# RWKV triangles inverted from 16x16 substitution and 32x32 products, transposed by TensorE

## The chip, the core and the metric

The kernel runs on one core of one Trainium2 chip. TensorE multiplies matrices into PSUM, VectorE, ScalarE and GpSimd work elementwise, and SyncE issues the DMAs. The metric is the device time of one execution in microseconds. Shorter is better; the median of the runs is compared.

## The reference

The reference is one block of a hybrid model on 512 latent tokens and 256 context tokens of width 1024: a projection, three mixers (RWKV7 in both directions, a convolution, an mLSTM), a gated merge, and an MLP. The change concerns the RWKV mixer alone, which runs this recurrence for 8 heads of size 64, forward and backward, first over the context and then, from its state, over the latents:

```python
def step(S, inp):
    w_t, k_t, v_t, kk_t, a_t = inp[:5]
    S = (S * w_t[:, :, None, :]
         - jnp.einsum('bhvk,bhk->bhv', S, kk_t)[..., None] * (kk_t * a_t)[:, :, None, :]
         + v_t[..., None] * k_t[:, :, None, :])
    y = jnp.einsum('bhvk,bhk->bhv', S, inp[5]) if emit else None
    return S, y
```

## The kernel before

The recurrence is cut into 12 chunks of 64 tokens (8 latent, 4 context). Within a chunk the 64 updates are tied together by a 64x64 unit triangle of inner products, which the kernel inverts; a chunk's effect on the state is then a few matrix products. Two heads make a pair j (0 to 3); forward and backward direction lie in the lower and the upper 64 partitions of a tile.

For a pair, `ctx` and `lat` load the operands, `gram` forms the inner products and masks them, `transposed` turns the keys around, and `invert` inverts 48 triangles (2 directions, 2 heads, 12 chunks) at once. Each 64x64 triangle is handled as two diagonal blocks of 32x32 and one block off the diagonal. VectorE transposes the diagonal blocks so that the chunks lie along the free axis within each partition (L1012), solves them by 30 steps of substitution, two operations each (L1017, L1019), transposes what the off-diagonal products need (L1022, L1024), and transposes the result back (L1042); TensorE only forms the off-diagonal blocks (L1033, L1034, L1048, L1049), and ScalarE moves them out of PSUM.

`chain` walks the 12 chunks of a pair in 36 steps, three for each chunk: a product with the state (L1100), the product with the inverted triangle TT (L1106), and the product that makes the next state (L1115), with ScalarE copies between (L1104, L1109) and a sum on VectorE at the end (L1116). `output` forms the results (L1081, L1082).

`weave(j)` sets the order: at each step of `chain(j)` it asks for a number of pieces of the preparation of pair j + 1 (`lat`, with `gram` and `invert`, then `ctx` of pair j + 2; the table PACE says how many pieces, one piece ends at each `yield`), and for some three matmuls of the merge gates (`gates`, L512), 100 spread over the steps and 20 at the end. The chain has a raised priority, and the other pieces are tied behind the chain's last instruction. A scheduler then puts each engine's instructions into one order, which that engine follows. Three stages, j = 0, 1, 2, prepare the next pair; the fourth runs beside the conv branch's norm and the modulation weights. Pair 0 is prepared earlier, between the heads of the mLSTM (`front`, `back`, whose operations are at L262 and from L788 to L858).

The gate products need weights that are split in two: ScalarE rounds (L152) and GpSimd forms the difference (L153). GpSimd also scales the chain's state (L1113) and the keys (L995).

## Time and profile before

| | us |
|---|---|
| median of 3 runs | 1371.11 |
| lowest, highest | 1370.52, 1717.46 |
| profiled execution | 1377.12 |
| its span, first to last instruction | 1375.3 |
| busy in it: TensorE, VectorE, GpSimd, ScalarE | 1252.9, 849.2, 585.7, 511.8 |

The profile is one execution, some 6 us above the median. Busy time is the union of an engine's records; records of matmuls overlap, since the next one starts before the last one has left the array. A window's row gives the busy time of each engine in that stretch, the granted TensorE clock as a share of full speed, and the load of the DMA engines. The chain of waits is followed back from the last instruction, at each step to whatever released it.

### The profile page before, as it was taken

Reading aid. Unit: us, or ns where it says so; the run is one execution under the profiler, and the core shown is the slowest. Engines: PE = TensorE matmul, PEld = TensorE weight load, DVE = VectorE, ACT = ScalarE, POOL = GpSimd, SP = SyncE. Lnnn points to the kernel's source line nnn. Section 1 sums busy time; section 2 is a strip of 40 time slices with the busy share of each in tenths; the row PEclk is TensorE's granted clock in tenths of the full one; section 3 lists DMA queues with packets and bytes.
Section 4 is the critical chain, followed back from the end, with each engine's and each line's share of the span. In section 5 each row is a group of like instructions: output and inputs, shape, how many; then the busy total and the mean of one; then the engine's idle time right before and its main releaser. Section 6 shows DMA issues by size and latency. Waiting matters only on the chain.

```text
span 1375.3 us, 21700 instructions
## 1 busy us (share of the span) xinstructions
PE 1252.9 (91%) x8004; PEld 969.6 (71%) x8004; DVE 849.2 (62%) x1509; ACT 511.8 (37%) x1048; POOL 585.7 (43%) x547
## 2 busy tenths in 40 slices
PE   6999989786999886999899988889999999999997
PEld 1587877565888775667566665667888878888886
DVE  2599588889266993797977857678366534300202
ACT  4434556632222231243342444422354444322322
POOL 0443334426755441332433435533456544444442
PEclk9999999898999997999998998999999999999999
DMA  9221588732633314323431244787434433433422
GB/s 375 65 69 58 134 270 255 246 104 62 186 99 97 111 64 120 110 93 101 143 110 49 85 145 136 259 263 249 131 112 156 142 100 95 153 104 96 131 95 89
DMA packets 101457, 187.85 MB, mean 137 GB/s; under 512 B 10708, under 2 KB 29396, under 8 KB 100328
## 3 DMA queue, kind: packets, MB, share of 16 engines
q1 hardware_dynamic: 101352, 186.47, 42.9%
q8 instruction: 63, 1.03, 0.3%
q14 instruction: 42, 0.34, 0.1%
HBM read 148.64 MB, written 29.40 MB: 129 GB/s over the span
## 4 chain that ended last, share of the span: by engine, by line
PE 45%; DVE 14%; DMA 5%; issue 3%; ACT 1%; POOL 1%; SPq 0%; DVEq 0%; POOLq 0%; ACTq 0%
PE pt L1268 16%; PE pd L1337 13%; PE dg L512 5%; DMA wad<-wada 4%; DVE N L1019 3%; DVE tmp L1017 2%; PE pg L973 2%; PE ch L1100 1%; PE pd L682 1%; DVE N L1012 1%; PE ch L1106 1%; DVE accm L608 1%; PE dl L262 1%; PE pbk L998 1%; PE ch L1115 1%
## 5 line engine op out<-in xcount | busy, mean ns | idle before, releaser
L153 POOL TENSOR_TENSOR wlo<-raw,whi 128x512 fp32r<-128x512 f32 x296 | 435.5, 1477 | 555.5 <-ACT whi L152 488.9
L152 ACT CAST whi<-raw 128x512 fp32r<-128x512 f32 x296 | 182.0, 618 | 318.7 <-PE pt L1268 118.8
L262 PE MATMUL dl<-hh,wlo 128*128 128x512 f32 (+1 forms) x368 | 149.7, 407 | 10.8 <-POOL wlo L153 10.8
L262 PE MATMUL dl<-hh,whi 128*128 128x512 f32 (+1 forms) x368 | 151.4, 412 | 2.7 <-ACT kT L758 1.9
L262 PE MATMUL dl<-hl,whi 128*128 128x512 f32 (+1 forms) x368 | 148.5, 403 | 0.0
L1337 PE MATMUL pd<-h2l,whi 128*128 128x512 f32 (+1 forms) x272 | 103.3, 381 | 0.7 <-POOL h2l L1320 0.7
L1337 PE MATMUL pd<-h2h,wlo 128*128 128x512 f32 (+1 forms) x272 | 102.7, 379 | 0.0
L1337 PE MATMUL pd<-h2h,whi 128*128 128x512 f32 (+1 forms) x272 | 101.5, 380 | 0.2 <-ACT h2h L1317 0.2
L1363 DVE TENSOR_TENSOR x<-pt,modb 128x512 f32<-128x512 f32 x8 | 5.5, 690 | 154.7 <-PE pt L1268 154.7
L1268 PE MATMUL pt<-whi,h1h 128*128 128x512 f32 x256 | 99.6, 389 | 0.0
L1268 PE MATMUL pt<-whi,h1l 128*128 128x512 f32 x256 | 99.6, 389 | 0.0
L1268 PE MATMUL pt<-wlo,h1h 128*128 128x512 f32 x256 | 99.1, 389 | 0.0
L262 PEld LDWEIGHTS dl<-hh,wlo 128*128 128x128 f32 (+1 forms) x368 | 70.7, 192 | 26.0 <-POOL wlo L153 11.2
L262 PEld LDWEIGHTS dl<-hh,whi 128*128 128x128 f32 (+1 forms) x368 | 71.2, 193 | 18.6 <-ACT kT L758 2.1
L262 PEld LDWEIGHTS dl<-hl,whi 128*128 128x128 f32 (+1 forms) x368 | 70.8, 192 | 15.2 <-issue 1.5
L608 DVE SCALAR_TENSOR_TENSOR accm<-wad,sc,accm 128x512 f32<-128x512 f32 x56 | 59.1, 1056 | 35.2 <-DMA wad<-wada 34.6
L1113 POOL TENSOR_TENSOR sps<-SV,PL 64x128 f32<-64x128 f32 x88 | 40.0, 454 | 85.1 <-DVE SV L1116 81.9
L1341 DVE TENSOR_TENSOR relu<-relu 128x512 f32<-128x512 f32 x32 | 38.9, 1218 | 55.8 <-ACT relu L1340 55.7
L512 PE MATMUL dg<-hl,whi 128*128 128x512 f32 x144 | 66.5, 462 | 0.0
L512 PE MATMUL dg<-hh,whi 128*128 128x512 f32 x144 | 65.7, 456 | 0.0
L512 PE MATMUL dg<-hh,wlo 128*128 128x512 f32 x144 | 65.6, 456 | 0.0
L1019 DVE TENSOR_TENSOR N<-N,tmp 128x30 f32<-128x30 f32 (+14 forms) x120 | 58.1, 484 | 3.0
(389 smaller groups left out, 2792.3 us busy)
## 6 DMA issues: line engine op xcount, KB each, us to landing
raw<-wblk SPq DMA_DIRECT2D x296, 256.0 KB, 2.9
wad<-wada SPq DMA_DIRECT2D x64, 256.0 KB, 4.0
wada<-wada SPq DMA_DIRECT2D x8, 1024.0 KB, 13.4
BK<-kb SPq DMA_DIRECT2D x16, 384.0 KB, 5.2
sp_bk<-BK SPq DMA_DIRECT2D x8, 768.0 KB, 5.2
BK<-sp_bk SPq DMA_DIRECT2D x8, 768.0 KB, 4.1
sp_g<-gt SPq DMA_DIRECT2D x24, 256.0 KB, 2.0
sp_al<-al SPq DMA_DIRECT2D x8, 640.0 KB, 4.6
```

The costliest lines, as they stand in the source:

```text
L152: A.copy(hi[:, :], raw[:, :])
L153: G.tensor_tensor(lo[:, :], raw[:, :], hi[:, :], ALU.subtract)
L262: PE.matmul(ps_[0:M, :], lhsT=w[:, ko:ko + M], rhs=x[seg][:, k, :], start=(n == 0), stop=(n == 3 * KT - 1))
L512: yield lambda w=w, x=x, k=k, ko=ko, n=n: PE.matmul(ps[:, :], lhsT=w[:, ko:ko + P], rhs=x[:, k, :], start=(n == 0), stop=(n == 3 * KT - 1))
L608: V.scalar_tensor_tensor(o, t[:, :], sc[:, k, 0:1], o, ALU.mult, ALU.add)
L973: PE.matmul(ps[hf, i, :, :], lhsT=BK[dd, c, x, :], rhs=al[:, c] if lat else AL[d][dd, 8 + c:9 + c, :], start=True, stop=True)
L1017: V.tensor_tensor(tv, N[:, s + 1:32, s:s + 1].to_broadcast([P, n, s]), N[:, s:s + 1, 0:s].to_broadcast([P, n, s]), ALU.mult)
L1019: V.tensor_tensor(N[:, s + 1:32, 0:s], N[:, s + 1:32, 0:s], tv, ALU.add)
L1113: last["Pool"] = G.tensor_tensor(sps[hf], SV[d][hf, c, :, :], PL[hf, c, :].unsqueeze(2).to_broadcast([64, 2, CH]), ALU.mult)
L1268: PE.matmul(pss[i][:, :], lhsT=x[:, k, ts_], rhs=w[:, :], start=(k == 0 and n == 0), stop=(k == nk - 1 and n == 2))
L1337: PE.matmul(ps[:, ts_], lhsT=w[:, ko:ko + P], rhs=x[:, k, ts_], start=(k == 0 and n == 0), stop=(k == 7 and n == 2))
L1341: V.tensor_tensor(t[:, :], t[:, :], t[:, :], ALU.mult)
```

## The change

The substitution now runs on 16x16 blocks, in 14 steps of two operations, and on all of them at once. N gets its transposed form by TensorE: products of the masked Gram blocks with slices of the identity into PSUM, and two ScalarE copies into N. The inverted 16x16 diagonal blocks come back in the same way, once as D and once transposed as Dt. GpSimd multiplies LT by a mask that clears the 16x16 diagonal blocks. With L the rest of the 32x32 block, I + L D is formed in PSUM and multiplied by D, which gives the inverse of the 32x32 block; its transpose is formed by further products. The blocks off the 32x32 diagonal follow by the same two products as before. Copies from PSUM are shared between ScalarE and VectorE.

`gram` now collects in one PSUM bank the products of both directions that stay in their own half of the partitions (`own`), and in a second bank those that go to the other half (`oth`); the first are masked by one operation over 128 partitions, into LT, which holds the former LR as its second half. The masks change with it. The first pair now uses the bank "m" as the second bank, later pairs a bank of the chain's pool. The tables PACE, DENSE and EXTRA stay as they are, and `invert` and `gram` yield fewer pieces. LR, TN and most of tmp go, and the mLSTM's result yc takes a buffer of gbc in turn. The constants loaded at the start grow by 64 columns.

```diff
@@ -46,7 +46,7 @@
 NBLK = 148
-CONST_ORDER = [("ident", 128), ("bones", 128), ("gmf", 128), ("gmb", 128), ("nmf", 128), ("nmb", 128)]
+CONST_ORDER = [("ident", 128), ("bones", 128), ("gmo", 128), ("gmx", 128), ("dm", 64), ("nmf", 128), ("nmb", 128)]
@@ -88,15 +88,15 @@
     SY.dma_start(par[:, :], params)
-    cst = K.tile([P, 512], F32, name="cst")
-    SY.dma_start(cst[:, :], consts[:, 0:512])
+    cst = K.tile([P, CO["nmf"]], F32, name="cst")
+    SY.dma_start(cst[:, :], consts[:, 0:CO["nmf"]])
     def CN(name):
-        return cst[:, CO[name]:CO[name] + 128]
+        return cst[:, CO[name]:min(CO[name] + 128, CO["nmf"])]
@@ -854,7 +854,7 @@
             PE.transpose(pt[:, c * 128:(c + 1) * 128], ht[:, c, :], ident)
-        yc = S.tile([P, NT], F32, tag="yc", name="yc")
+        yc = S.tile([P, NT], F32, tag="gbc", name="yc", bufs=2)
@@ -878,16 +878,16 @@
             self.BK = [S.tile([P, NCH, 2, CH], F32, name=f"BK{h}") for h in range(2)]
-        self.LT.append(S.tile([P, 32, CH], F32, name=f"LT{i}"))
-        self.tc.nc.gpsimd.memset(self.LT[i][:, 24:32, :], 0.0)
+        self.LT.append(S.tile([P, 2, 24, CH], F32, name=f"LT{i}"))
                 self.AL[d].append(S.tile([P, 20, CH], F32, name=f"AL{d}{i}{h}"))
-            self.LR.append(S.tile([P, 8, CH], F32, name=f"LR{i}{h}"))
         if i == 0:
-            self.tmp = S.tile([P, 256], F32, name="tmp")
-            self.N = S.tile([P, 32, 32], F32, name="N")
-            self.TN = S.tile([P, 32, 32], F32, name="TN")
+            self.tmp = S.tile([P, 112], F32, name="tmp")
+            self.N = S.tile([P, 1056], F32, name="N")
+            self.tc.nc.gpsimd.memset(self.N[:, :], 0.0)
+            self.D, self.Dt = (S.tile([P, 24, 32], F32, name=x) for x in ("D", "Dt"))
@@ -895,15 +895,15 @@
         PS = self.ea.enter_context(tc.tile_pool(name="psa", bufs=1, space=PSUM, side="right", reuse_waits="tile"))
-        self.PS, self.PG = PS, [PS]
-        self.AL, self.LR, self.LT, self.BKt = [[], []], [], [], []
+        self.PS, self.PG = PS, (PS, "m")
+        self.AL, self.LT, self.BKt = [[], []], [], []
         self.PSC = self.es.enter_context(tc.tile_pool(name="psb", bufs=1, space=PSUM, reuse_waits="tile"))
-        self.PG.append(self.PSC)
+        self.PG = (self.PSC, "g")
@@ -954,41 +954,40 @@
     def gram(self, j, h, quarters):
         nc, HF = self.tc.nc, self.HF
         V, PE = nc.vector, nc.tensor
-        AL, LR, BKt, BK = self.head(j, h)
+        AL, BKt, BK = self.head(j, h)
         LT = self.LT[j % 2]
-        gm = [self.CN("gmf"), self.CN("gmb")]
         for c4 in quarters:
+            lat = c4 < 2
+            w = 2 if lat else 1
+            own, oth = (pool.tile([P, 4, w, CH], F32, tag=tag, name="pg") for pool, tag in ((self.PS, "g"), self.PG))
+            for i in range(4):
+                c = c4 * 4 + i
+                for x, ps in enumerate((own, oth)):
+                    for d in range(2):
+                        dd, hf = HF[d], HF[(d + x) % 2]
+                        al = AL[d][dd, 0:16, :].rearrange("p (x c) t -> p c x t", x=2)[:, c] if lat else AL[d][dd, 8 + c:9 + c, :]
+                        PE.matmul(ps[hf, i, :, :], lhsT=BK[dd, c, x, :], rhs=al, start=True, stop=True)
+            mo, mx = (self.CN(n)[:, (2 - w) * CH:2 * CH].rearrange("p (x t) -> p x t", t=CH).unsqueeze(1).to_broadcast([P, 4, w, CH])
+                      for n in ("gmo", "gmx"))
+            g = h * 12 + c4 * 4
+            dst = LT[:, ::-1, g:g + 4, :] if lat else LT[:, 0:1, g:g + 4, :]
+            V.tensor_tensor(dst.rearrange("p x c t -> p c x t"), own[:, :, :, :], mo, ALU.mult)
+            yield
             for d in range(2):
-                dd, od = HF[d], HF[1 - d]
...
-                yield
+                od = HF[1 - d]
                 if lat:
                     dst = AL[d][od, 0:16, :].rearrange("p (x c) t -> p c x t", x=2)[:, c4 * 4:c4 * 4 + 4]
                 else:
                     dst = AL[d][od, 16:20, :].unsqueeze(2)
-                V.tensor_tensor(dst, ps[od], m_[od], ALU.mult)
+                V.tensor_tensor(dst, oth[od], mx[od], ALU.mult)
                 yield
     def transposed(self, j, h, quarters):
         nc = self.tc.nc
         A, G, PE = nc.scalar, nc.gpsimd, nc.tensor
-        AL, LR, BKt, BK = self.head(j, h)
+        AL, BKt, BK = self.head(j, h)
         for c4 in quarters:
             cs = slice(c4 * 4, c4 * 4 + 4)
             pl = self.PL[:, j, cs, h:h + 1].unsqueeze(3).to_broadcast([P, 4, 2, CH])
@@ -1000,61 +999,93 @@
             yield
     def invert(self, j):
-        nc, S, PS = self.tc.nc, self.S, self.PS
+        nc = self.tc.nc
         V, A, G, PE = nc.vector, nc.scalar, nc.gpsimd, nc.tensor
         LT = self.LT[j % 2]
-        N, TN, tmp = self.N, self.TN, self.tmp
...
-            V.transpose(N[qs] if d == 0 else N[qs].rearrange("p a b -> p b a"), src)
+        LTf = LT.rearrange("p x g t -> p (x g) t")
+        N, tmp, D, Dt, ident = self.N, self.tmp, self.D, self.Dt, self.ident
+        Q = [(q, q // 2, 32 * (q % 2), slice(32 * q, 32 * q + 32)) for q in range(4)]
+        Nf = N[:, 0:1024].rearrange("p (a b) -> p a b", b=32)
+        Nd = N.rearrange("p (u x) -> p u x", u=2)[:, :, 0:512].rearrange("p u (a b) -> p u a b", b=32)[:, :, :, 0:16]
+        tags = iter(("g", "m") * 20)
+        psum = lambda shape: self.PS.tile([P] + shape, F32, tag=next(tags), name="px")
+        pn = psum([2, 16, 16])
+        for t in range(32):
+            u = t // 16
+            for q, d, o, qs in Q:
+                PE.matmul(pn[qs, u, t % 16, :], lhsT=LTf[qs, 0:32, o + t], rhs=ident[qs, 32 * q + 16 * u:32 * q + 16 * u + 16],
+                          start=True, stop=True)
+            if t == 15:
+                yield
+        A.copy(Nd[0:64], pn[0:64])
+        A.copy(Nd[64:128].rearrange("p u a b -> p u b a"), pn[64:128])
+        G.tensor_tensor(LTf[:, 0:24, :], LTf[:, 0:24, :], self.CN("dm")[:, 0:CH].unsqueeze(1).to_broadcast([P, 24, CH]), ALU.mult)
+        yield
+        for s in range(1, 15):
+            n = 15 - s
+            tv = tmp[:, 0:2 * n * s].rearrange("p (u t j) -> p u t j", u=2, t=n)
+            V.tensor_tensor(tv, Nd[:, :, s + 1:16, s:s + 1].to_broadcast([P, 2, n, s]),
+                            Nd[:, :, s:s + 1, 0:s].to_broadcast([P, 2, n, s]), ALU.mult)
+            V.tensor_tensor(Nd[:, :, s + 1:16, 0:s], Nd[:, :, s + 1:16, 0:s], tv, ALU.add)
             yield
-        for s in range(1, 31):
...
-            V.tensor_tensor(N[:, s + 1:32, 0:s], N[:, s + 1:32, 0:s], tv, ALU.add)
+        G.memset(N[:, 0:1024:33], 1.0)
+        for x, dst in enumerate((D, Dt)):
+            for u in range(2):
+                pd = psum([16, 24])
+                for i in range(16):
+                    t = 16 * u + i
+                    for q, d, o, qs in Q:
+                        qg = slice(32 * q, 32 * q + 24)
+                        PE.matmul(pd[qs, i, :], lhsT=Nf[qg, t, :] if (d + x) % 2 else Nf[qg, :, t],
+                                  rhs=ident[qg, 32 * q:32 * q + 24], start=True, stop=True)
+                A.copy(dst[:, :, 16 * u:16 * u + 16].rearrange("p g t -> p t g"), pd[:, :, :])
+                yield
+        for g8 in (0, 12):
+            gs = slice(g8, g8 + 12)
+            px = psum([12, 32])
+            for q, d, o, qs in Q:
+                iq = ident[qs, 32 * q:32 * q + 32]
+                PE.matmul(px[qs, :, :], lhsT=iq, rhs=iq.unsqueeze(1).to_broadcast([32, 12, 32]), start=True, stop=False)
+            for i in range(12):
+                for q, d, o, qs in Q:
+                    PE.matmul(px[qs, i, :], lhsT=LTf[qs, g8 + i, o:o + 32], rhs=D[qs, g8 + i, :], start=False, stop=(i == 11))
+            A.copy(D[:, gs, :], px[:, :, :])
             yield
-        G.memset(N.rearrange("p a b -> p (a b)")[:, 0:1024:33], 1.0)
...
-            xs.append(TN[:, g8:g8 + 12, :])
+            pt, pu = psum([12, 32]), psum([12, 32])
+            for i in range(12):
+                for q, d, o, qs in Q:
+                    PE.matmul(pt[qs, i, :], lhsT=D[qs, g8 + i, :], rhs=Dt[qs, g8 + i, :], start=True, stop=True)
+                for q, d, o, qs in (Q[0], Q[3]):
+                    PE.matmul(pu[qs, i, :], lhsT=Dt[qs, g8 + i, :], rhs=D[qs, g8 + i, :], start=True, stop=True)
+            for q, d, o, qs in Q:
+                (A.copy if q % 2 else V.tensor_copy)(LTf[qs, gs, o:o + 32], pt[qs])
+            for q, d, o, qs in (Q[0], Q[3]):
+                (A.copy if q else V.tensor_copy)(Dt[qs, gs, :], pu[qs])
+            yield
+            px = psum([12, 32])
             for i in range(12):
                 g = g8 + i
-                PE.matmul(px[32:64, i, :], lhsT=LT[0:32, g, 32:64], rhs=TN[0:32, g, :], start=True, stop=True)
-                PE.matmul(px[64:96, i, :], lhsT=LT[96:128, g, 0:32], rhs=TN[96:128, g, :], start=True, stop=True)
-            A.copy(xs[x][32:64], px[32:64])
-            A.copy(xs[x][64:96], px[64:96])
+                PE.matmul(px[32:64, i, :], lhsT=LTf[0:32, g, 32:64], rhs=Dt[0:32, g, :], start=True, stop=True)
+                PE.matmul(px[64:96, i, :], lhsT=LTf[96:128, g, 0:32], rhs=Dt[96:128, g, :], start=True, stop=True)
+            A.copy(Dt[32:64, gs, :], px[32:64])
+            V.tensor_copy(Dt[64:96, gs, :], px[64:96])
             yield
-        for q in range(4):
...
-            py = self.off_diagonal(x)
+            py = psum([12, 32])
             for i in range(12):
                 g = g8 + i
-                PE.matmul(py[0:32, i, :], lhsT=xs[x][32:64, i, :], rhs=LT[32:64, g, 32:64], start=True, stop=True)
-                PE.matmul(py[96:128, i, :], lhsT=xs[x][64:96, i, :], rhs=LT[64:96, g, 0:32], start=True, stop=True)
-            A.copy(LT[0:32, g8:g8 + 12, 32:64], py[0:32])
-            A.copy(LT[96:128, g8:g8 + 12, 0:32], py[96:128])
+                PE.matmul(py[0:32, i, :], lhsT=Dt[32:64, g, :], rhs=LTf[32:64, g, 32:64], start=True, stop=True)
+                PE.matmul(py[96:128, i, :], lhsT=Dt[64:96, g, :], rhs=LTf[64:96, g, 0:32], start=True, stop=True)
+            A.copy(LTf[0:32, gs, 32:64], py[0:32])
+            V.tensor_copy(LTf[96:128, gs, 0:32], py[96:128])
             yield
         if j == 0:
-            self.dump("TT", LT[:, 0:24, :])
-    def off_diagonal(self, x):
-        return self.PS.tile([P, 12, 32], F32, tag="mg"[x], name="px")
+            self.dump("TT", LTf[:, 0:24, :])
     def load(self, j, groups):
         nc, HF = self.tc.nc, self.HF
@@ -1079,14 +1110,14 @@
                     PE.matmul(o, lhsT=self.SV[d][:, c, h, :], rhs=self.AL[d][sl[h]][:, c, :], start=(d == 0), stop=False)
-                PE.matmul(o, lhsT=self.UU[:, c, h, :], rhs=self.LR[sl[h]][:, c, :], start=False, stop=True)
+                PE.matmul(o, lhsT=self.UU[:, c, h, :], rhs=self.LT[j % 2][:, 1, h * 12 + c, :], start=False, stop=True)
         V, A, G, PE = nc.vector, nc.scalar, nc.gpsimd, nc.tensor
-        UV, SV, TT, PL = self.UV, self.SV, self.LT[j % 2], self.PL[:, j]
+        UV, SV, TT, PL = self.UV, self.SV, self.LT[j % 2][:, 0], self.PL[:, j]
@@ -1459,12 +1490,13 @@
     i = np.arange(64)
     lt, le = (i[:, None] < i[None]).astype(f), (i[:, None] <= i[None]).astype(f)
-    gmf = np.block([[le, -lt], [le, lt]])
-    gmb = np.block([[le.T, lt.T], [le.T, -lt.T]])
+    gmo = np.block([[le, -lt], [le.T, -lt.T]])
+    gmx = np.block([[le.T, lt.T], [le, lt]])
+    dm = np.tile((i[:, None] // 16 != i[None] // 16).astype(f), (2, 1))
     bones = np.kron(np.eye(2), np.ones((64, 64))).astype(f)
     i = np.arange(128)
     nmf = np.where(i[:, None] <= i[None], 0.0, NEG).astype(f)
-    cs = {"ident": np.eye(P, dtype=f), "bones": bones, "gmf": gmf, "gmb": gmb, "nmf": nmf, "nmb": nmf.T}
+    cs = {"ident": np.eye(P, dtype=f), "bones": bones, "gmo": gmo, "gmx": gmx, "dm": dm, "nmf": nmf, "nmb": nmf.T}
     consts = np.concatenate([cs[n] for n, _ in CONST_ORDER], 1).astype(f)
     rowp = np.stack([g["b_ada"][0, 2048:3072], g["b_ada"][0, 5120:6144], g["g_final"]], 0)
     res = {
```

## Rows read from the trace of the kernel before

**Rows 1.** Windows by stage: length, PE, PEld, DVE, ACT, POOL busy, clock, DMA.

```profile
441.00:515.00 74.00, 63.68 (x509) 53.14 (x508) 70.28 (x163) 20.53 (x39) 32.82 (x33) 0.95 0.30 93
515.00:541.00 26.00, 16.39 (x84) 13.68 (x83) 12.05 (x50) 2.84 (x5) 5.40 (x8) 0.83 0.29 97
541.00:628.00 87.00, 80.94 (x923) 57.31 (x925) 66.18 (x128) 30.17 (x92) 28.91 (x43) 0.90 0.42 121
628.00:719.00 91.00, 82.84 (x962) 58.36 (x959) 71.76 (x141) 34.53 (x99) 31.05 (x43) 0.92 0.34 104
719.00:803.00 84.00, 77.57 (x872) 54.58 (x873) 67.69 (x136) 31.50 (x93) 30.25 (x40) 0.92 0.26 78
```

**Rows 2.** The chain of waits from 541 to 803 us, shares by line.

```profile
by line: PE dg L512 24.7%; PE pg L973 12.1%; DVE N L1019 9.8%; DVE tmp L1017 7.3%; issue 5.6%; PE ch L1100 5.3%; PE ch L1106 4.1%; PE pbk L998 3.4%; DVE N L1012 3.3%; PE ch L1115 3.0%; DVE SV L1116 2.4%; PE py L1081 2.2%; DVE AL L984 1.8%; 
```

**Rows 3.** VectorE's groups in the whole run: line, shapes, count, busy, mean ns.

```profile
L1019 DVE TENSOR_TENSOR N<-N,tmp 128x30 f32<-128x30 f32 (+14 forms) x120 | 58.1, 484 | 3.0
...
L1017 DVE TENSOR_TENSOR tmp<-N 128x30 f32<-128x30 f32 (+14 forms) x120 | 49.7, 414 | 3.1
...
L1042 DVE STREAM_TRANSPOSE LT<-N 32x1024 f32<-32x1024 f32 x16 | 32.6, 2038 | 0.4
```

**Rows 4.** VectorE's groups by form, 541 to 803 us.

```profile
L1017 DVE TENSOR_TENSOR tmp<-N 128x84 f32<-128x84 f32 x6 | 1.5, 247 | 0.1
```

**Rows 5.** Timeline at 460.7 us, all engines: start, length, engine, line.

```profile
460.75 1.29 POOL L153 TENSOR_TENSOR wlo<-raw,whi 128x512 fp32r<-128x512 f32 x1 [1.93 <-ACT whi L152]
460.91 1.30 DVE L1017 TENSOR_TENSOR tmp<-N 128x150 f32<-128x150 f32 x1
```

**Rows 6.** Timeline of VectorE in the second stage, start and end of the inversion.

```profile
658.14 0.42 DVE L976 TENSOR_TENSOR LT<-pg,cst 64x256 f32<-64x256 f32 x1 [1.52 <-PE pg L973]
...
658.90 0.69 DVE L984 TENSOR_TENSOR AL<-pg,cst 64x512 f32<-64x512 f32 x1
659.61 3.90 DVE L1012 STREAM_TRANSPOSE N<-LT 32x1024 f32<-32x1024 f32 x2
...
705.40 8.43 DVE L1042 STREAM_TRANSPOSE LT<-N 32x1024 f32<-32x1024 f32 x4
```

**Rows 7.** TensorE's groups, 541 to 803 us.

```profile
L512 PE MATMUL dg<-hl,whi 128*128 128x512 f32 x115 | 53.5, 465 | 0.0
...
L973 PE MATMUL pg<-AL,BK 64*64 64x128 f32 (+1 forms) x576 | 38.1, 273 | 8.5 <-DVE AL L984 8.5
L1100 PE MATMUL ch<-SV,AL 128*64 128x64 f32 x296 | 25.2, 245 | 13.3 <-ACT UU L1119 8.8 <-DMA SV<-sp_v 4.4
```

**Rows 8.** Timeline of TensorE, first inversion: one row group, then two in turn.

```profile
499.25 0.31 PE L1033 MATMUL px<-TN,LT 32*32 32x32 f32 x4 [0.55 <-DVE TN L1022]
...
501.32 0.19 PE L1034 MATMUL px<-TN,LT 32*32 32x32 f32 x1
501.33 0.19 PE L1033 MATMUL px<-TN,LT 32*32 32x32 f32 x1
...
501.48 0.19 PE L1034 MATMUL px<-TN,LT 32*32 32x32 f32 x1
```

**Rows 9.** Timeline of TensorE, one batch of Gram products.

```profile
732.34 1.09 PE L973 MATMUL pg<-AL,BK 64*64 64x128 f32 x16
```

**Rows 10.** Timeline of TensorE at the end of the second stage.

```profile
715.69 0.32 PE L1106 MATMUL ch<-xc,LT 64*64 64x64 f32 x2
715.95 0.50 PE L512 MATMUL dg<-hh,wlo 128*128 128x512 f32 x1
716.28 0.39 PE L512 MATMUL dg<-hh,whi 128*128 128x512 f32 x1
716.51 0.40 PE L512 MATMUL dg<-hl,whi 128*128 128x512 f32 x1
```

**Rows 11.** Timeline of TensorE before the first woven stage.

```profile
536.37 1.15 PE L856 MATMUL pt<-cst,ht 128*128 128x128 f32 x4 [6.13 <-DVE ht L855]
541.91 1.24 PE L1100 MATMUL ch<-SV,AL 128*64 128x64 f32 x8 [4.39 <-DMA SV<-sp_v]
```

More of the change, by code (lines that the diff above doesn't have):

```diff
@@ L919, in head @@
         sl = (2 * j + h) % 4
-        return [self.AL[d][sl] for d in range(2)], self.LR[sl], self.BKt[sl], self.bk[j, h]
+        return [self.AL[d][sl] for d in range(2)], self.BKt[sl], self.bk[j, h]
     def ctx(self, j):
@@ L956, in gram @@
         V, PE = nc.vector, nc.tensor
-        AL, LR, BKt, BK = self.head(j, h)
+        AL, BKt, BK = self.head(j, h)
         LT = self.LT[j % 2]
-        gm = [self.CN("gmf"), self.CN("gmb")]
         for c4 in quarters:
-            for d in range(2):
-                dd, od = HF[d], HF[1 - d]
-                lat = c4 < 2
-                w = 2 if lat else 1
-                ps = self.PG[d % len(self.PG)].tile([P, 4, w, CH], F32, tag="g", name="pg")
-                al = AL[d][dd, 0:16, :].rearrange("p (x c) t -> p c x t", x=2) if lat else None
-                for i in range(4):
-                    c = c4 * 4 + i
-                    for x, hf in ((0, dd), (1, od)):
-                        PE.matmul(ps[hf, i, :, :], lhsT=BK[dd, c, x, :], rhs=al[:, c] if lat else AL[d][dd, 8 + c:9 + c, :],
-                                  start=True, stop=True)
-                m_ = gm[d][:, (2 - w) * CH:2 * CH].rearrange("p (x t) -> p x t", t=CH).unsqueeze(1).to_broadcast([P, 4, w, CH])
-                V.tensor_tensor(LT[dd, h * 12 + c4 * 4:h * 12 + c4 * 4 + 4, :], ps[dd, :, w - 1, :], m_[dd, :, w - 1, :], ALU.mult)
-                if lat:
-                    V.tensor_tensor(LR[dd, c4 * 4:c4 * 4 + 4, :], ps[dd, :, 0, :], m_[dd, :, 0, :], ALU.mult)
-                yield
@@ L1037, in invert @@
+            A.copy(Dt[32:64, gs, :], px[32:64])
+            V.tensor_copy(Dt[64:96, gs, :], px[64:96])
             yield
-        for q in range(4):
-            d, bl = q // 2, q % 2
-            qs = slice(32 * q, 32 * q + 32)
-            src = N[qs] if d == 0 else N[qs].rearrange("p a b -> p b a")
-            V.transpose(LT[qs, :, 32 * bl:32 * bl + 32].rearrange("p g t -> p t g"), src)
-            yield
-        for x, g8 in enumerate((0, 12)):
-            py = self.off_diagonal(x)
+            py = psum([12, 32])
```

14 lines of the change are left out of this document (removed).

## The prediction

> **What bounds the kernel now.** I read the windows by stage first, because the change touches one stretch only, 441 to 803 us: the first inversion runs in 441 to 541 beside the mLSTM heads, the three others in the three stages woven with the RWKV chain (541 to 628, 628 to 719, 719 to 803). Two things are to be seen in them [rows 1]. In 441 to 515 VectorE is busy 70.3 of 74 us and TensorE 63.7: there VectorE is the bound. In the three stages TensorE is busy 80.9 of 87, 82.8 of 91 and 77.6 of 84 us, and VectorE only 66 to 72: there TensorE has 20.7 us idle in all. Second, the chain of waits through the three stages: it lies on TensorE for the dense gates (24.7%), the Gram products (12.1%) and the RWKV chain, but the inversion's substitution on VectorE is next, 9.8 + 7.3% with 3.3% for the first transposes, some 53 of 262 us [rows 2]. So both engines hold the end in turn, and the change takes from the one and gives to the other. That is the whole question.
>
> **VectorE: what goes and comes, for one pair of heads (there are four).** The substitution now takes 120 + 120 operations in four inversions, (58.1 + 49.7)/4 = 27.0 us each, and 40 transposes of 32x1024 (L1012, L1042, L1022, L1024), 10 x 2.0 = 20.4 us each [rows 3]. These 47 us go. In come 14 steps of two operations whose length is 2s(15 - s), 80 elements on average: 28 x 0.25 us [rows 4] = 7 us, and 9 us with stretches such as now occur, where an operation with two SBUF inputs takes 1.30 us beside a GpSimd operation of 1.29 us [rows 5]. Ten evictions of 32x384 from PSUM come to VectorE, each between the 0.42 us of 64x256 and the 0.69 of 64x512 [rows 6], about 5 us. Gram masks: six operations for four chunks (0.42, again 0.42 and 0.69 us, twice) become three of 0.69 [rows 6]; four such groups and two of context chunks (four of 0.42 become three) make 15.6 us before and 10.8 after. Net: 47 - 14 + 5 = 38 us less VectorE for each pair.
>
> **TensorE: what comes.** One fp32 matmul is two records: three pairs have 288 Gram matmuls and 576 records [rows 7]. The new inversion has 128 transposing products into N, 256 back into D and Dt, 8 + 96 to form I + L D, 96 + 48 for the inverse and its transpose, and 96 as before: 728 matmuls, 1456 records, against 96 and 192. So 1264 more for each inversion. Their price is the largest unknown. The nearest rows have two row groups of the array in turn (L1034, L1033): five pairs start in 0.16 us (501.32 to 501.48), 0.032 for a pair and 0.016 for one record, and four records from a single row group come at about 0.03 to 0.04 each (they end within 0.31 us, one lasting 0.19) [rows 8]. A second row group was thus free. If four row groups run abreast as two do, a record costs 0.008, 10 us in all; if two is the most, 0.016, 20 us. I take 14, since no row has four row groups at once, and some of the new weights (all of N's, half of D's) are read with a stride, which no row shows. The rule of the Trainium skill that bears on this speaks against the change: in "TensorEngine Tiling (Array Packing)", Gotcha 1, different row tiles cannot use the same PSUM bank at the same time, and all four quadrants here write one bank. The rows of the trace differ from it, for their two row groups write one bank and start 0.01 us apart; by the rule the price would be 0.032 us a record, 40 us an inversion.
>
> Two smaller terms. The 192 Gram records of a pair cost (1.09 - 0.27)/15 = 0.054 us each, with 0.27 for the last [rows 7, 9]; with the halves of the array now taken in turn between them they may cost half: 0 to 5.2 us back, I take 2.6. Each batch in another tile shape costs its neighbours 0.1 us on entry and 0.1 on leaving: a gate matmul follows another after 0.23 us (716.28 to 716.51), but after 0.33 where the first came right behind a chain product (715.95 to 716.28) [rows 10]; I take as much on the way out. Four batches become 14 or, where the chain cuts them, more: 2 to 5 us, I take 3. Net TensorE: +14 - 2.6 + 3 = 14 us for each pair, between 7 (10 - 5.2 + 2) and 25.
>
> **What else is moved.** ScalarE: 8 copies of 32x384 become some 18 of that size and more, 5 us more at VectorE's price for such; it is busy 30 to 35 us a stage [rows 1]. GpSimd gets the mask of the 16x16 blocks, 128x1536, three times the 1.29 us of 512 columns [rows 5], 4 us; behind it on its queue stand the weight differences of the gate products and the state scaling of the chain, and the first substitution steps may stand still beside it. It comes once a stage, 0 to 4 us; I count 1 inside the fill below. The result yc now takes one of the two gbc buffers: the next head's second gbc load waits for yc's store, and on SP's queue the weight loads stand behind it. A store of that size and the load behind it take some 3 us each by the 4.39 us in which the chain's first product waits for a state load [rows 11]; three weight blocks are loaded ahead, so 0 to 3 us, in the first window alone. The wider constant load hides under the start. The Gram products of one batch now need both banks free at once; TensorE has gate products between, and if none is ready a batch waits for two masks, 1.4 us.
>
> **The sum, on the profiled execution (1377.1 us, span 1375.3, so 1.8 around it; its median run is 1371.1, 6 us lower, and I carry differences over).** Window 441 to 541: TensorE idle 19.9 us [rows 1], new work 14. The last 11 us are a tail: 6.13 us for the layer norm of the last head on VectorE and 4.39 for the state load [rows 11]; with VectorE free the first should move ahead of the last gate products, the second stays. I take 20 - 14 = 6 us gained (18 to -10). Three stages: what TensorE needs, worked out from counts and pitches, is 346 gate matmuls x 0.23 = 80, 576 Gram x 0.054 = 31, 848 of the chain x some 0.054 = 46 [rows 7], the smaller groups about 33, and 290 changes of tile shape x 0.1 = 29: 219 of 262 us (an estimate; the idle 20.7 and waits shorter than a matmul's own 0.2 to 0.4 us are the rest). New need 219 + 3 x 14 = 261. Against it: in these stages the granted clock is 0.90 to 0.92, so some 45 of 262 us run at 1.2 GHz and the rest at 2.4, the low stretches following on TensorE's waits; if these waits go, perhaps 10 us come back. At a fill of 0.96 the stages then last 251/0.96 = 262 us: no change. The waits that vanish are paid for by the work that fills them. Total: -6, 1371 - 6 = **1365 us**.
>
> **Rivals.** (A) VectorE decides. The inversion lasts from 659.6 to past 713.8 us in the second stage, its last transposes alone 8.4 us [rows 6], and the next chain waits for it with its second product until 715.69 [rows 10]. With four row groups abreast TensorE gets only +7 a pair: (219 + 21 - 12)/0.95 = 240, 22 us off the stages, and 12 off the first window: 1337. For it: 53 us of the chain of waits. Against it: during that last wait TensorE runs gate products back to back [rows 10], so the time is not empty. (B) TensorE becomes the bound: at 0.016 us a record and broken batches, +25 a pair, (219 + 75 - 12)/0.95 = 297, 35 us on the stages and 6 on the first window: 1412. It decides from about 19 us of net TensorE work a pair, past which no wait is left to be filled. (C) Row groups that write one bank wait for each other, 0.032 us a record, 40 us an inversion: stages (219 + 120 - 12)/0.95 = 344, first window +20: about 1470. The pairs in [rows 8] are against it. (It is the rule on PSUM banks above.) (D) The change doesn't do what it says: the inversion is not shorter, since its some 14 hops between TensorE, ScalarE and VectorE each queue behind gate and chain work at 2.5 to 3 us, and the next chain waits as now; TensorE's work then fits in the waits that stay: 1371.
>
> **How the numbers follow.** My forecast 0.43, A 0.27, D 0.10, B 0.16, C 0.04. Two per cent, 27 us, is about what a measurement here can tell from no change: faster 0.27, same 0.53, slower 0.20. The range, 1330 to 1402, takes in the forecast, D and A's 1337 and leaves out B's 1412 and C.
>
> **What would show it.** VectorE's busy time in the run falls by some 150 us (849 to about 700). The stages' 262 us stay within 15; if A holds they fall to 240 with the new matmuls at 0.008 us a record, if B holds the pitch is 0.016 and TensorE's idle time in the stages drops to under 5 us. A stretched weight load, or GpSimd's mask holding the chain, would make the prediction wrong upward; a clock that stays at 2.4 GHz through the stages, downward.

## Result

The changed kernel takes 1488.23 us (median of 4 runs, 1486.48 to 1492.53), the kernel before 1373.38 us beside it; the ratio is 1.0848, 95% interval 1.0808 to 1.0889: 8.5% slower. One of the four runs of the kernel before took 1717 us in a slower state of the chip, and the ratio leaves it out. The forecast was 1365 with a range of 1330 to 1402. The profiled execution took 1486.48 us; its span and busy times, then the five stretches that answer to [rows 1] (the first inversion, the rest of the first window, the three woven stages; columns as there):

```profile
span 1484.4 us, 31643 instructions
...
PE 1382.4 (93%) x13060; PEld 1090.1 (73%) x13060; DVE 726.0 (49%) x1325; ACT 540.4 (36%) x1088; POOL 587.2 (40%) x550
```

```profile
410.00:491.00 81.00, 69.66 (x1716) 60.74 (x1714) 38.72 (x108) 23.60 (x43) 27.39 (x27) 0.85 0.18 58
491.00:563.00 72.00, 61.44 (x331) 51.74 (x331) 31.52 (x115) 17.68 (x34) 31.90 (x35) 0.92 0.36 117
563.00:679.00 116.00, 112.74 (x2187) 87.01 (x2188) 32.39 (x79) 37.95 (x102) 31.60 (x42) 0.81 0.30 83
679.00:805.00 126.00, 121.76 (x2192) 94.69 (x2189) 35.47 (x95) 41.02 (x108) 34.17 (x44) 0.78 0.28 82
805.00:928.00 123.00, 121.15 (x2169) 94.45 (x2169) 34.16 (x93) 40.39 (x106) 33.81 (x42) 0.76 0.19 61
```

VectorE's busy time in a stage is halved, TensorE is idle for 1.9 to 4.2 us of each, and the granted clock has gone from 0.90 to 0.92 down to 0.76 to 0.81. I measure a stage from one chain's first pair of products with TT for the second head (it waits for the whole inversion) to the next chain's. Before, these stand at 544.5, 629.4, 718.9 and 807.2 us, now at 563.1, 679.3, 804.5 and 928.1: stages of 84.9, 89.4 and 88.3 us have become 116.2, 125.2 and 123.6. The chain of waits there, by line, against [rows 2]: VectorE's substitution has left the front, and the new products have come in (L1019 into N, L1044 into D and Dt, L1056 forms I + L D, L1062 the inverse). The chain's three products now stand at L1131, L1137 and L1146, Gram at L970.

```profile
by line: PE dg L512 28.3%; PE px L1044 9.0%; PE pg L970 8.6%; PE ch L1137 8.1%; PE ch L1131 7.8%; PE ch L1146 7.6%; PE px L1019 4.1%; PE pbk L997 3.1%; PE py L1112 2.9%; PE px L1056 2.8%; PE px L1062 2.1%; DMA BK<-sp_bk 1.7%; DVE tmp L1031 
```

For a balance I give each TensorE record the time from its start to the next record's start. The three stages together grew from 262.7 to 365.0 us, by 102.3: the inversion's products from 10.8 to 89.5 (+78.7), the chain's products, whose number is the same, from 54.9 to 89.3 (+34.4), all the rest -10.8, nearly all of it the gates, behind whose records the waits fall from 16 to 5 us. The first window is 18.6 us longer and what follows the fourth chain's start 11.8 shorter (there VectorE's waits for the weights of wad fall from 34 to 21 us): 102.3 + 18.6 - 11.8 = 109.1, the difference of the spans. The medians lie some 8 us further apart, since the profile before was 6 us above its median and this one 2 below. The same two groups by their busy time, in three windows each (PE is the first number); first the inversion's products after and before, then the chain's:

```profile
sum 365.00, PE 96.80 PEld 76.30 DVE 15.78 ACT 31.55; mean PE 32.27 PEld 25.43 DVE 5.26 ACT 10.52
```

```profile
sum 263.00, PE 11.54 PEld 10.31 ACT 11.29; mean PE 3.85 PEld 3.44 ACT 3.76
```

```profile
sum 365.00, PE 102.83 PEld 73.67 DVE 18.98 ACT 49.04; mean PE 34.28 PEld 24.56 DVE 6.33 ACT 16.35
```

```profile
sum 263.00, PE 61.92 PEld 44.50 DVE 19.00 ACT 47.28; mean PE 20.64 PEld 14.83 DVE 6.33 ACT 15.76
```

TensorE's and VectorE's groups, answering to [rows 7] (563 to 928 us) and [rows 3] (whole run; count, busy, mean ns):

```profile
L1044 PE MATMUL px<-cst,N 24*32 24x24 f32 x1536 | 37.7, 221 | 0.6 <-DVE N L1033 0.6
L970 PE MATMUL pg<-AL,BK 64*64 64x128 f32 (+1 forms) x576 | 36.9, 277 | 3.0 <-DMA BK<-sp_bk 3.0
...
L1131 PE MATMUL ch<-SV,AL 128*64 128x64 f32 x288 | 34.1, 274 | 2.1 <-ACT UU L1150 2.1
...
L1019 PE MATMUL px<-cst,LT 32*32 32x16 f32 x768 | 17.5, 210 | 0.2 <-issue 0.2
```

```profile
L1031 DVE TENSOR_TENSOR tmp<-N 128x28 f32<-128x28 f32 (+6 forms) x56 | 25.8, 460 | 15.3 <-ACT N L1024 14.0
...
L1033 DVE TENSOR_TENSOR N<-N,tmp 128x28 f32<-128x28 f32 (+6 forms) x56 | 19.9, 355 | 1.4
```

Now the second stage in detail. From 743 to 767 us TensorE is busy all the time and its clock is 0.50 of full speed, 1.2 GHz:

```profile
743.00:767.00 24.00, 24.00 (x502) 19.61 (x501) 2.14 (x8) 7.61 (x24) 3.01 (x8) 0.50 0.08 25
```

The timeline of TensorE shows what it does there and before, here and at three other places (start, length, line, count; a run's pitch is its length less the last record's 0.2, at the low clock 0.22, divided by the count less one):

```profile
410.05 1.89 PE L1019 MATMUL px<-cst,LT 32*32 32x16 f32 x120
...
741.77 0.86 PE L1044 MATMUL px<-cst,N 24*32 24x24 f32 x48
...
744.97 0.43 PE L1044 MATMUL px<-cst,N 24*32 24x24 f32 x12
745.32 0.69 PE L1146 MATMUL ch<-UV,BKt 128*64 128x64 f32 x4
745.94 0.74 PE L1044 MATMUL px<-cst,N 24*32 24x24 f32 x36
746.61 0.69 PE L1131 MATMUL ch<-SV,AL 128*64 128x64 f32 x4
...
789.46 0.55 PE L1056 MATMUL px<-D,LT 32*32 32x32 f32 x40
```

No gate product stands between them: four chain records, a dozen new ones, four chain records, three dozen new ones. Four chain records take 0.62 us (745.32 to 745.94) where they take 0.38 at the full clock between the same neighbours. Stretched weights are those read with a stride (L1019, and half of L1044): these products come every 0.014 us at the full clock (410.05, 741.77) and every 0.015 at the low one (745.94); unstretched ones at the full clock every 0.009 (789.46). The inversion's products come in 42 to 50 separate runs a stage, before in 3 or 4.

The clock is not the whole of the chain's +34.4 us. Of its 840 records in the three stages, 496 now stand in groups next to new products. At the full clock these cost 0.098 us each (176 of them) and at the low one 0.156 (320), against 0.053 at the full clock away from them. By these prices the cuts make some 22 us (496 x 0.044), and the clock about as much (320 x 0.058, and 76 low records elsewhere x 0.055, less 2 us that it cost before); some 9 us of waits and other losses that the chain had before are gone. This split is an estimate.

### The profile page after: what moved, and what is told of

The parts are those of the page before. It is cut to its first block, busy times and chain, and to the rows that moved or that the text cites. A ratio compares the mean times of both kernels' runs of the same rounds, so it can differ in the third digit from the quotient of the medians.

```text
span 1484.4 us, 31643 instructions
## 1 busy us (share of the span) xinstructions
PE 1382.4 (93%) x13060; PEld 1090.1 (73%) x13060; DVE 726.0 (49%) x1325; ACT 540.4 (36%) x1088; POOL 587.2 (40%) x550
## 4 chain that ended last, share of the span: by engine, by line
PE 63%; DVE 11%; DMA 5%; issue 2%; ACT 2%; POOL 1%; SPq 0%; DVEq 0%; POOLq 0%; ACTq 0%
PE pt L1299 15%; PE pd L1368 12%; PE dg L512 7%; PE dl L262 5%; PE pg L970 3%; PE px L1044 3%; DMA wad<-wada 3%; DVE cy L291 2%; PE ch L1131 2%; PE ch L1137 2%; PE ch L1146 2%; PE px L1019 1%; PE dc L262 1%; PE pd L682 1%; DVE tmp L1031 1%
## 5 line engine op out<-in xcount | busy, mean ns | idle before, releaser
L153 POOL TENSOR_TENSOR wlo<-raw,whi 128x512 fp32r<-128x512 f32 x296 | 424.0, 1437 | 592.7 <-ACT whi L152 520.4
L1147 DVE TENSOR_TENSOR SV<-ch,sps 64x128 f32<-64x128 f32 x88 | 25.3, 288 | 129.8 <-PE ch L1146 115.6
L608 DVE SCALAR_TENSOR_TENSOR accm<-wad,sc,accm 128x512 f32<-128x512 f32 x56 | 54.3, 970 | 24.2 <-DMA wad<-wada 23.4
```

The lines of the kernel that those rows point to most:

```text
L153: G.tensor_tensor(lo[:, :], raw[:, :], hi[:, :], ALU.subtract)
L608: V.scalar_tensor_tensor(o, t[:, :], sc[:, k, 0:1], o, ALU.mult, ALU.add)
```

## The experiments

Theory 1: TensorE's work, at the price that its new products have and make for others, sets the time. Theory 2: the latency of Gram and inversion, with its hops between engines each queued behind other work, sets it, and TensorE is merely full of what is left over. Ratios are against the kernel before on the same chip.

**Transposing left out.** One product with 256 or 384 columns in place of 16 (for N, and likewise for D and Dt):

```diff
-        for t in range(32):
-            ...PE.matmul(pn[qs, u, t % 16, :], lhsT=LTf[qs, 0:32, o + t], rhs=ident[...])
+        for u in range(2):
+            ...PE.matmul(pn[qs, u, :, :], lhsT=LTf[qs, 0:32, o + 16 * u], rhs=ident[...] broadcast to [32, 16, 16])
```

> Leaves out the transposing itself: the 384 transposing products of an inversion (128 into N, 256 into D and Dt, 768 records) become 24 of 256 or 384 columns that repeat one slice, so N, D and Dt hold other numbers; every copy, wait and hop stays. Theory 1 (TensorE is the bound through the new products): in the stage 681 to 805 us these 768 records hold TensorE for 10.8 + 5.2 us, their substitutes should need some 3; with four inversions 50 us go, and perhaps 10 to 20 more from the clock: 1418 to 1440 us. Theory 2 (the hops of the inversion, each behind gate products, set the stage): the hops stay, 1475 to 1490 us.

1399.04 us, 1.0208 (1.0151 to 1.0265): of the loss of 8.5%, 2.1% are left, less than theory 1 expected. The clock is back as well (columns as in the windows above), and the inversion's products come in 22 to 29 runs a stage:

```profile
553.00:644.00 91.00, 88.09 (x1466) 63.22 (x1462) 33.05 (x79) 37.09 (x102) 31.61 (x42) 0.98 0.39 107
644.00:745.00 101.00, 95.52 (x1470) 67.29 (x1468) 37.81 (x95) 40.10 (x108) 34.30 (x44) 0.93 0.29 92
745.00:836.00 91.00, 86.20 (x1451) 61.72 (x1449) 35.27 (x91) 38.68 (x105) 33.63 (x42) 0.98 0.27 86
```

Yet even so the inversion lasts 62 to 70 us in the three stages from its first to its last instruction, 55 to 66 before and 87 to 96 as changed: the hops and products that are left take as long as all that VectorE saves.

**Gram alone.** `gram`, masks and yc as changed; `invert` with N, TN and tmp as before, LT and the former LR in one tile of 52 groups:

```diff
-        self.LT.append(S.tile([P, 2, 24, CH], F32, name=f"LT{i}"))
+        self.LT.append(S.tile([P, 52, CH], F32, name=f"LT{i}"))
```

> The new Gram masking alone, with the substitution on 32x32 blocks and the VectorE transposes of the kernel before. Theory 1: the loss is all in the inversion, so this is the kernel before with 5 us less VectorE work a pair, 1355 to 1375 us. Rival: the Gram batches that need two banks free at once carry part of the loss; then over 1390 us.

1370.88 us, 0.9993 (0.9962 to 1.0023): neither gain nor loss. The loss comes with the new inversion.

**VectorE transposes.** 16x16 substitution and 32x32 products stay:

```diff
-        pn = psum([2, 16, 16]) ... A.copy(Nd[64:128]..., pn[64:128])
+        V.transpose(Nf[qs] if d == 0 else Nf[qs].rearrange("p a b -> p b a"), LTf[qs, 0:32, o:o + 32]...)
-        pd = psum([16, 24]) ... A.copy(dst[...], pd[:, :, :])
+        V.transpose(D[qs]..., Nf[qs]...)
+        V.transpose(Dt[qs]..., D[qs, 0:24, :]...)
```

> As changed, but N, D and Dt are made by VectorE transposes (12 for an inversion, some 22 us of VectorE) in place of the 384 transposing products and their six copies. Theory 1: 768 records leave TensorE, 16 us a stage and what the clock gives back with it; VectorE has some 15 us a pair less than in the kernel before; 1380 to 1430 us. Theory 2: six hops fewer but VectorE's own 22 us in their place, 1440 to 1480 us.

1452.26 us, 1.0614 (1.0548 to 1.068): above theory 1's range and inside theory 2's. The inversion lasts 76 to 80 us, and now TensorE is idle 14 to 16 us in each stage of 104.4 to 109.7:

```profile
553.00:657.00 104.00, 89.95 (x1426) 66.19 (x1424) 52.25 (x92) 33.12 (x96) 31.96 (x44) 0.87 0.31 85
657.00:767.00 110.00, 94.67 (x1421) 68.88 (x1420) 54.75 (x107) 34.57 (x99) 32.83 (x45) 0.88 0.28 87
767.00:876.00 109.00, 93.45 (x1386) 67.04 (x1385) 55.66 (x104) 35.38 (x101) 35.07 (x44) 0.87 0.24 77
```

In this form TensorE's work no longer fills the stage, and the run fits theory 2: the latency, with 22 us of transposes on VectorE in it. So theory 1 alone does not cover every form: where TensorE is relieved and VectorE loaded, the latency is the limit.

**Pieces asked for more slowly.** `PACE = [2] * 36`:

> As changed, but the preparation is asked for at two pieces in each of the 36 chain steps instead of 4, 3, 2 and 0, so that gate products stand between the new products. Theory 1 with the clock as its second half: the 55 us a stage at 1.2 GHz fall to under 35, the stage loses 8 to 12 us: 1450 to 1465 us. If the low clock comes from the small products wherever they stand: 55 us stay, 1480 to 1500. Theory 2: the inversion starts later and ends later, over 1500 us.

1471.4 us, 1.0726 (1.0653 to 1.0799), in none of the three ranges. The edit did not do what it was meant to: the scheduler still put no gate products among the new ones, and 137 us of the three stages ran at 1.2 GHz against 157 as changed.

**Unstretched weights.** Other slices, the same number and shapes:

```diff
-lhsT=LTf[qs, 0:32, o + t]
+lhsT=LTf[qs, t % 24, 0:32]
-lhsT=Nf[qg, t, :] if (d + x) % 2 else Nf[qg, :, t]
+lhsT=Nf[qg, t, :]
```

> As changed, but the weights of the 384 transposing products are read without a stride (other slices of LT and N, so N, D and Dt hold other numbers); their number, size and order stay. If the stretched weight loads make the pitch of 0.0142 us a record seen at 410 to 416 us, against 0.008 with unstretched weights at 789 us, the 768 records of an inversion lose some 5 us at the full clock and up to 8 with the low one: 20 to 35 us in all, 1450 to 1468 us, and the weight loads fall from 0.14 to 0.11 us. If the stride does not matter, 1483 to 1493 us.

1474.64 us, 1.0743 (1.0683 to 1.0802): 14 us, less than the 20 of the one reading and more than the other's nothing. L1019's weight loads fell from 143 to 113 ns. TensorE's timeline shows why no more came of it, first at the full clock, then at the low one, where the pitch is that of stretched weights, (0.53 - 0.22)/21 = 0.015 us:

```profile
703.18 0.44 PE L1019 MATMUL px<-cst,LT 32*32 32x16 f32 x32
...
725.81 0.53 PE L1044 MATMUL px<-cst,N 24*32 24x24 f32 x22
```

**Gates first.** In `weave`:

```diff
                 if f:
-                    self.paced(last, f, ("PE",))
+                    with self.tc.high_priority(1500):
+                        self.paced(last, f, ("PE",))
```

> As changed, but gate products get a raised priority (below the chain's), so that three of them stand between any two chain steps and the new products come in runs of some 13 between them. The work is the same. Theory 1 with the clock: in the third stage 54 us at 1.2 GHz fall to under 20, chain and new products lose some 15 us a stage, 1430 to 1455 us. If the low clock follows the small products wherever they stand, it stays at 45 or more: 1480 to 1500 us. Theory 2 (latency of the inversion): the transposing products take twenty chain steps instead of ten and the inversion ends later, over 1500 us.

1464.3 us, 1.0655 (1.0596 to 1.0713), 9 us above the range of theory 1 with the clock. Gate products now stand between the chain's steps, and four chain records between new products take 0.38 us again (743.83 to 744.21); eight that stand together take no more (741.97 to 742.36), so a cut in the chain's own group doubles its price:

```profile
741.97 0.46 PE L1146 MATMUL ch<-UV,BKt 128*64 128x64 f32 x8
742.36 0.50 PE L512 MATMUL dg<-hh,wlo 128*128 128x512 f32 x1
...
743.25 0.65 PE L1044 MATMUL px<-cst,N 24*32 24x24 f32 x32
743.83 0.45 PE L1131 MATMUL ch<-SV,AL 128*64 128x64 f32 x4
744.21 0.29 PE L1044 MATMUL px<-cst,N 24*32 24x24 f32 x6
744.42 0.45 PE L1131 MATMUL ch<-SV,AL 128*64 128x64 f32 x4
744.80 0.50 PE L512 MATMUL dg<-hh,wlo 128*128 128x512 f32 x1
```

```profile
566.00:677.00 111.00, 99.73 (x2187) 75.03 (x2188) 32.54 (x80) 37.34 (x102) 31.50 (x42) 0.88 0.32 95
677.00:792.00 115.00, 106.48 (x2193) 78.62 (x2191) 34.56 (x95) 39.64 (x107) 34.15 (x44) 0.92 0.28 82
792.00:901.00 109.00, 102.12 (x2169) 76.42 (x2167) 34.17 (x92) 38.91 (x106) 33.59 (x42) 0.91 0.22 68
```

The low clock falls from 157 to 66 us of the three stages, and in the second one, which the expectation counts as the third, from 55 to 18, as expected; the time did not follow in full. The chain's time falls from 89.3 to 52.3, about what it was before (54.9); its busy time in the three windows, against 102.83 and 61.92 above, is back as well:

```profile
sum 335.00, PE 62.02 PEld 44.27 DVE 18.98 ACT 47.18; mean PE 20.67 PEld 14.76 DVE 6.33 ACT 15.73
```

The 34.4 us of the balance go, but the edit moved two things at once: the clock, and the number of runs, which fell from 42 to 50 a stage to 22 to 31. The inversion's products shrink little (104.8 us with 22.6 of waits in them, against 89.5 with 3.5): those with stretched weights have nearly the same pitch at either clock, and TensorE now waits 7 to 11 us a stage, mostly for their hops. The stages lose 30 us together; in the profile the first window and what follows the stages give 14 of it back, and the medians lie 24 us apart.

**yc beside ht.** `yc = S.tile([P, NT], F32, tag="ht", name="yc")`:

> As changed, but the result yc shares the buffer of ht in place of gbc's. If the chain of store, load and masks at 476 to 485 us (yc, then 2.6 us of store, 3.7 us of load, then gbc) sets the start of the RWKV chain, the first window loses 3 to 8 us: 1480 to 1485 us. If TensorE's work sets it, no change: 1486 to 1492 us.

1487.47 us, 1.0827 (1.0773 to 1.0881): no cost of the shared buffer can be seen.

**Half the old substitution.** In the kernel before, `for s in range(1, 31, 2)`:

> The kernel before with every second of the 30 substitution steps left out (other numbers in N): some 13 us less VectorE work in each inversion and nothing more for TensorE. It shows what a shorter substitution is worth at most. If VectorE's latency decides the three stages, each loses 8 to 13 us: 1335 to 1350 us. If TensorE's work is the floor (83 of 89 us in the second stage), each loses at most its idle 5 to 8 us: 1350 to 1365 us.

1383.24 us, 1.0102 (1.0065 to 1.014): slower, which neither reading had. The inversions last 42 to 47 us instead of 55 to 66 and end 16 to 24 us before the first product of the next chain, and the stages are 92.6, 95.5 and 87.5 us, not shorter than before:

```profile
537.00:630.00 93.00, 81.90 (x985) 59.55 (x985) 56.68 (x102) 32.12 (x95) 29.42 (x43) 0.89 0.35 105
630.00:725.00 95.00, 81.79 (x915) 58.24 (x914) 58.20 (x110) 32.31 (x96) 30.81 (x43) 0.87 0.32 95
725.00:813.00 88.00, 77.12 (x860) 55.00 (x859) 55.66 (x102) 32.16 (x96) 29.18 (x40) 0.90 0.28 88
```

VectorE's busy time fell by some 12 us a stage, TensorE's stayed at 77 to 82 us. TensorE is idle for 11 to 13 us a stage, more than before. Some 24 of these 35 us are the chain's own: its first products wait 14.4 us for ScalarE's copy into UU and 9.7 for VectorE's sum into SV, where before the copy took 8.8. So once the inversion is early, the chain's own hops seem to hold the stage, a limit that neither theory has; why the scheduler's new order leaves more of them bare is not settled. The low clock rose too, from 42 to 62 us of the three stages, and may hide a few us. What matters: in the kernel before this shorter substitution gained nothing.

**Products nobody reads.** In the kernel before, after the substitution:

```diff
+        for x in range(2):
+            for u in range(2):
+                pd = self.PS.tile([P, 16, 24], F32, tag="mg"[u], name="pd")
+                for i in range(16):
+                    ...PE.matmul(pd[qs, i, :], lhsT=N[qg, t, :] if (q // 2 + x) % 2 else N[qg, :, t], rhs=self.ident[...])
```

> The kernel before, untouched, with 256 transposing products (512 records) added to each inversion after its substitution, in the form of the changed kernel's products into D and Dt; nobody reads them, so no hop and no wait of the inversion hangs on them. Theory 1: TensorE is the bound of the kernel before too, so they cost their own 512 x 0.0145 us and some ten changes of tile shape of 0.25 us, 8 to 11 us an inversion, and more if the clock falls beside them: 1395 to 1430 us. Theory 2 (hops and latency made the loss): up to 1380 us, since 8 of 88 us a stage are idle.

1428.76 us, 1.0451 (1.0417 to 1.0485), at the upper end of theory 1's range: 58 us for 2048 records, 0.028 us each, twice their pitch. Not all of it is their own time: the low clock in the three stages rose from 42 to 83 us, and they stand in TensorE's queue and in the two banks ahead of the off-diagonal products, so the inversion got longer too (70 to 78 us). That no hop hangs on them was not quite so; theory 2's limit of 1380 is still far off.

**Gates first in the kernel before.** The same edit there:

> The kernel before with the raised priority for the gate products that was tried on the changed kernel. If gate products between the small ones keep the clock up here too, the 40 us at 1.2 GHz in the three stages shrink and 5 to 15 us go: 1355 to 1365 us, which would beat both kernels. If the low stretches of the kernel before come from its waits, the order changes little or delays the inversion: 1370 to 1400 us.

1376.85 us, 1.0035 (0.9993 to 1.0076): no difference, as the second reading had it. In the profile the low clock takes 65 us of the three stages, against 42: gate products put first did not keep the clock up here. No kernel run here beats the kernel before.

**Both edits on the changed kernel.**

> The changed kernel with both edits tried before: gate products first, and the weights of the transposing products unstretched (other numbers). Alone the second bought 14 us only, for in the low clock stretched and unstretched products have the same pitch of some 0.0145 us. With the clock up 768 records should come at 0.0087: 4.5 us less for each of four inversions, 1440 to 1450 us. If the changes of tile shape are most of the price, 1455 to 1465 us.

1450.99 us, 1.0633 (1.0585 to 1.0681), 1 us above the range for the pitch. By the medians it is 13 us below gates first alone, but the two ratios, 1.0633 and 1.0655, each against the kernel before on its own chip, overlap almost wholly, so this gain is not clear of the noise. 108 runs of the inversion's products stay in the three stages.

**Half the gates.** `DENSE = (50, 50, 50, 110)`, `EXTRA = (10, 10, 10, 300)`:

> As changed, but with 60 gate products in each of the three stages in place of 120; the others follow in the fourth stage and behind it, where they lengthen the run, so the stages are to be read, not the total. The inversion and the chain are untouched. Theory 1 (TensorE's work sets the stage): each stage, now 116, 125 and 124 us, loses the time of 60 gate products, some 20 us, and comes to 97 to 106 us with TensorE idle for under 8 us. Theory 2 (the latency of Gram and inversion sets it): the stages stay over 112 us and TensorE is idle for 12 us or more in each.

1495.16 us in all; the stages are 109.1, 105.0 and 116.7 us, with TensorE idle for 9.4, 3.1 and 6.1 us:

```profile
561.00:671.00 110.00, 100.64 (x2137) 78.23 (x2138) 33.08 (x80) 34.00 (x95) 25.10 (x37) 0.73 0.26 73
671.00:776.00 105.00, 101.90 (x2127) 80.19 (x2123) 34.17 (x94) 36.23 (x100) 27.72 (x39) 0.78 0.26 72
776.00:892.00 116.00, 109.88 (x2110) 84.37 (x2110) 33.16 (x92) 35.28 (x98) 27.27 (x37) 0.71 0.16 51
```

The second is theory 1's. The first lies between the two, and the third is as long as theory 2 said but without its 12 us of idle time; both lose 7 us and not 20. 174 us ran at 1.2 GHz against 157, which may have eaten part of it. That the latency is close behind is likely, not shown.

**Half the new substitution.** In the changed kernel, `for s in range(1, 15, 2)`:

> As changed, with every second of the 14 substitution steps left out (other numbers in N): 14 VectorE operations less in each inversion, its path is some 5 to 8 us shorter, TensorE's work is the same. If TensorE's work sets the stages, no change: 1482 to 1495 us. If the inversion's latency sets them, three stages lose 5 to 8 us each: 1464 to 1475 us.

1472.93 us, 1.074 (1.0696 to 1.0784): the time lies in the latency's range, but only half of the gain comes from the stages. They lost 5.1, 0.6 and 2.4 us, where 5 to 8 each were expected, and the first window lost 7. The run with yc beside ht, which leaves the inversion alone, has stages up to 1.7 us away from those of the changed kernel, so 0.6 and 2.4 say little. The latency has a part in the first window and the first stage; in the second and third stage it is not to be seen.

## Why the prediction was wrong

**The step that failed** is "Net TensorE: +14 - 2.6 + 3 = 14 us for each pair", with its bounds of 7 and 25. It measured some 26 us of the inversion's products a stage (89.5 - 10.8 = 78.7 in three), with almost nothing off for Gram (11.0 us a stage against 11.6). Two parts of the term were mis-sized. First the price of a record: 0.008 for four row groups abreast is right where weights are unstretched and the clock is full (0.009), but 512 of the 768 transposing records have stretched weights and hold all 768 to 0.014, near rival B's 0.016. Second the changes of tile shape: 14 batches were counted, the chain cut them into 42 to 50 runs, and a run of six records takes 0.21 us (744.21 to 744.42 in the gates-first run) where the pitch makes it 0.08.

**The clock** was the second failure: "the low stretches following on TensorE's waits; if these waits go, perhaps 10 us come back". TensorE's idle time halved, from some 20 to 9.4 us, and the low clock rose from 42 to 157 us of the three stages. In the second stage it fell at 743.0 us, with no wait ahead and no gate product since 736.6, and rose at 770.3, after gate products had come back at 766.9. The gates-first run has the same work with gate products between and 66 us at the low clock. In the kernel before the same edit did not help, so this holds for the changed kernel's mix. The clock is about half of the chain's +34.4 us, by the estimate above; the other half is the cuts, for which the forecast had 3 us a pair, all neighbours together.

**The overlap** was the third: "the waits that vanish are paid for by the work that fills them". The sum let 251 us of need, 32 more than before, fit into the same 262 us. All work but the inversion's and the chain's products gave back 10.8 us in the three stages, a third of that.

**VectorE** did nearly as said: 849.2 to 726.0 us, 31 a pair where 38 were worked out (the substitution takes 45.7/4 = 11.4 us and not 9). That this was worth nothing is what the halved substitution in the kernel before suggests, with the chain's hops taking the inversion's place; rival A fell with it, and the "53 of 262 us" of the chain of waits in [rows 2] were not time to be won.

**The first window** was to gain 6 us and lost 18.6: its inversion's products hold TensorE for some 33 us instead of 5 (9.5 of the 33 are waits), and the tail of layer norm and load stayed (6.1 us of wait at 554 us, and the load, as in [rows 11]).

**The rivals.** B had the mechanism, TensorE past the point where waits can pay; its 1412 lacked the 42 to 50 runs a stage and the clock. C's 1470 came nearest, by luck and for the wrong reason: row groups that write one bank do not wait for each other (0.009 us a record at 789 us). The Trainium skill's rule on PSUM banks, on which it rested, is not borne out by this. D was right that the inversion would not be shorter. GpSimd's mask took 3.44 us against 4, and yc's buffer nothing that can be seen.

**Open** are why the halved substitution made the kernel before 1% slower, how much the chain's own hops set, and how the loss, above all that of the first window and the first woven stage, divides between TensorE's work and the inversion's latency.

## What to carry to other kernels

Before work is moved to the busiest engine, ask what the relieved engine's time was worth: halving the old substitution is a one-line run, and it gained nothing. Price many small products by the pitch with their own weight stride, by how often other work will cut them into runs, and by what their neighbours lose when the clock falls; a record came every 0.009 us in one place, and the run with products nobody reads lost 0.028 us for each. A chain of waits that names an engine says who came last, not that the others had nothing to do.

## What the hardware showed

- Four row groups writing one PSUM bank, each its own partitions, start 0.007 us apart and come to 0.009 us a record at the full clock (789.46 us).
- Weights read with a stride of 256 bytes load in 143 ns instead of 113 (L1019 as changed, and with unstretched weights), and raise that pitch to 0.014 us at the full clock. The Trainium skill, "Advanced Engine Details and Errata", section "SBUF Cachelines", says that reads which hit another 16-byte line each time are slower; the trace agrees. At the low clock the pitch is some 0.015 us with and without the stride (745.94 us, and 725.81 with unstretched weights).
- TensorE's granted clock stayed at 1.2 GHz for 24 us in which the engine never waited (743 to 767 us); it ran the small tiles of chain and inversion there, and no gate product before 766.9.
- Four chain records between new products took as long at the full clock, 0.38 us, as eight that stood together, 0.39 (gates first, 743.83 and 741.97 us).
- The first operation of the substitution in the second stage took 1.94 us beside GpSimd's mask of 3.44, the next ones 0.2.
